# Gate's output row built through DRAM instead of on TensorE, later products with B, and two more tiles turned by VectorE and DMA

## The chip, the cores and the metric

The kernel runs on one core of a Trainium2 chip. The metric is the device time of one execution in microseconds (us). Five engines work beside each other, each through its own queue in order: TensorE (PE; its weight loads are listed as PEld), VectorE (DVE), ScalarE (ACT), GpSimd (POOL) and SyncE (SP), which here only issues DMAs. SBUF is the on-chip memory with 128 partitions; PSUM holds what TensorE accumulates.

## The reference

One layer of a hybrid trunk. 256 context tokens and 256 latent tokens are normalized, modulated and projected; one part of the projection feeds a bidirectional state-space scan (SSD), another a spatial-gating MLP. Both results go through one output projection, are normalized again, scaled by `g_post` and by the modulation's `gate`, and added to the input. Cut to what matters here:

```python
shift, scale, gate = split(silu(c) @ w_ada + b_ada, 3)
xbc = silu(dwconv(z[..., :4096]))          # x: 2048, B: 1024, C: 1024
xh, Bm, Cm = xbc as 32 heads x 64, 8 groups x 128, 8 groups x 128
# per group g and direction, chunks of 128 tokens
states = einsum('bckgn,bckgr,bckgrp->bcgrpn', Bc, decay_to_end, xdt)
CB     = einsum('bcqgn,bckgn->bcgqk', Cc, Bc)
y_diag = einsum('bcgqk,bcgrqk,bckgrp->bcqgrp', CB, Lmat, xdt)
y_off  = einsum('bcqgn,bcgrpn,bcqgr->bcqgrp', Cc, h_starts, exp(acs))
...
out = rmsnorm(mix_out(...), g_post)
x = x + gate[:, None] * out
```

## The kernel before

All products that need float32 accuracy are made of three matmuls: each weight is split into a rounded part (`hi`, by ACT, L87 and L543) and the rest (`lo`, by DVE, L88 and L549), and so is the activation (`hhi`, `hlo`).

**Stages.** First the modulation and the first seven tiles of the projection, while the normalized input is being made (to about 120 us in the profile). Then the loop over `REST`: 25 further tiles of 128 channels of x, B and C. Then 16 blocks of the projection for the latent tokens only (v, u, the two gates; L1219 to L1221, tile `pa`), then the output projection (`pm`, `pq`) and a tail.

**The 32 tiles.** Group g of the scan uses tiles 4g and 4g+1 (x), 4g+2 (B) and 4g+3 (C, latent tokens alone, so 256 columns where the others have 512). Tiles 0 to 3, 12, 13 and 15 are computed in the first stage and wait in PSUM or in `zq`. For the others PE fills one of two PSUM banks of `acp` (tile `psx`): 48 matmuls, 3 for each of 16 k. When a tile is complete, `conv_tile` reads the bank: ACT makes the first tap (L608), DVE the other four (L624, eight instructions for x and B, four for C), ACT the SiLU (L627). With two banks, a tile cannot start before DVE's last tap on the tile two before it. The names `xbc9`, `psx10` and so on carry the tile's number.

**Turning a tile.** x, B and the scan's result y have to be turned from channel-major to token-major. `by_pe` decides how. Either PE transposes four blocks of 128 by 128 into PSUM and ACT copies them (`ptx`, `ptb`, `pty`); or `turn` lets DVE transpose blocks of 32 by 32 (L739) and writes the result to DRAM (`Dx`, `Db`, `Dy`), and `turned` reads it back in four DMAs (`xk`, `bk`, `yz`, L747), all from SP's queue. Before, group 0 and, in group 7, everything but its first x tile go by PE.

**A group's tail.** `plan_tile` for a C tile plans the rest of the group: products of C with B (`pcb`) and states (`psc`, `psl`: B with the weighted x, `xw` and `xl`, from POOL) at +6, masks on DVE (`cbb`, `cbf`), start states (`hs`: ACT, then POOL, then DVE, L891), `M` and `E` per chunk (POOL, DVE), the product of C with the states (`pso`) at +12, `yo` (DVE), POOL's additions to y (L935), the diagonal product (`psy`) at +16, its turning (`yc`, `Dy`, `yz`) and the last addition. The next group's exponents (`E<-R`, L828) follow at +17; when they are read, `row_load` fetches the next `R`, a broadcast of 1 MB from `acs` in DRAM, from POOL's queue.

**What sets the order.** In the loops the order on PE, DVE, ACT and POOL is the program's own: `later(dt, fn)` puts a step into a list with a due time, and `pump(dt)` moves a clock on and issues what is due. A 512-column tile moves the clock by 10.4 units, eight times 1.3, each time after six matmuls; a 256-column tile by 5.2. `late` puts a group's tail off: 11 units where B is turned by DMA (14 for group 3). SP's queue and everything from the second latent block on are ordered by the framework's scheduler.

**Gate.** `gate_tile` (DVE) makes the 16 columns of gate, 128 values each. `gate_bcast` turns them into a row on all 128 partitions, `G`: it loads `g_post` as a broadcast, transposes gate on PE (`psgt`, L1095), splits it into two parts and spreads it in four matmuls (`pg`, L1105) with DVE's diagonal `gd` before and a product with `G` behind each. `G` is used at the very end (`o_gate`).

Of the kernel before, what the change touches and what calls it, by code (L numbers as in the profile page):

```python
# [20 lines left out]
NGRP = 8

FIRST = (0, 1, 2, 3, 12, 13, 15)
REST = tuple(i for i in range(32) if i not in FIRST)
NST = len(FIRST)
WST = 64 + NST * P

# [20 lines left out]
def tile_hybrid_ssd_mlp(  # L48
# [7 lines left out]
    pcols: bass.AP,  # L56
    dtp: bass.AP,
    dskip: bass.AP,
    gpost: bass.AP,
    gv: bass.AP,  # L60
    wst: bass.AP,
    wxbc: bass.AP,
# [5 lines left out]
    nc = tc.nc  # L68
# [5 lines left out]
    cpool = ctx.enter_context(mkpool(name="cpool", bufs=1))  # L74
# [21 lines left out]
    y = ypool.tile([P, 4, 2, 512], F32, tag="big16", name="y")  # L96
# [32 lines left out]
    bab = stp.tile([P, KT, 2], F32, name="bab")  # L129
    nc.vector.tensor_scalar(bab[:, :, 0], pc[:, C_BADA + 16 : C_BADA + 32], 1.0, None, op0=ALU.add)  # L130
    nc.vector.tensor_copy(bab[:, :, 1], pc[:, C_BADA : C_BADA + 16])
    gate = cpool.tile([P, 48], F32, name="gate")
    nc.gpsimd.memset(gate, 0.0)
    cpool.tile([P, 64], F32, name="cpad")

# [22 lines left out]
    zq = (yseg(2), yseg(3), yseg(7)[:, 0:256])  # L158
# [13 lines left out]
    def spt(shape, name):  # L172
        return sps.tile(shape, F32, tag="s", name=name)
# [10 lines left out]
    cb, cbj = (yseg(2), yseg(3)), yseg(0)  # L184
# [151 lines left out]
    for k in range(KT):  # L336
# [7 lines left out]
        g = k % 4  # L344
        nc.tensor.matmul(pss[32 * g : 32 * g + 32, :], lhsT=ones[:, 0:32], rhs=sq, start=k < 4, stop=k >= KT - 4)
        if g == 3:
# [7 lines left out]
                     start=True, stop=True)  # L354
# [161 lines left out]
    drp = ctx.enter_context(mkpool(name="drp", bufs=1, space=bass.MemoryType.DRAM))  # L516
# [204 lines left out]
    def row_load(g):  # L721
        if g >= NGRP:
            return
        R = cv1.tile([P, 4, 2, 2, P], F32, tag="R", name=f"R{g}")
        nc.gpsimd.dma_start(R.rearrange("p h d c q -> p (h d c q)"),
                            acs[4 * g : 4 * g + 4, :].rearrange("h x -> (h x)").unsqueeze(0).partition_broadcast(P))
        rows_[g] = R
# [5 lines left out]
        return ap.rearrange("p (h q) -> p h q", h=4)  # L733

    def by_pe(g, what):
        return g == 0 or g == NGRP - 1 and what != "x0"

    def turn(T, src, nm):
        nc.vector.transpose(T.rearrange("p (b g c) -> p g b c", b=4, g=4), src.rearrange("p (g b c) -> p g b c", g=4, b=4))  # L739
# [84 lines left out]
    def ssd_min(g, c):  # L824
        R = rows_[g]
        if c == 0:
            gs_.setdefault(g, {})["E"] = cv1.tile([P, 2, 4, P], F32, tag="E", name=f"E{g}")
        nc.vector.tensor_tensor(gs_[g]["E"][:, c], R[:, :, 0, c, :], R[:, :, 1, c, :], op=ALU.min)  # L828
        if c == 1:
            row_load(g + 1)  # L830

    def ssd_e(g):
        E = gs_[g]["E"]
# [140 lines left out]
    LAND = 4.5  # L974

    def plan_tile(i, src, d0=0.0, ds=5.2, tx=7.0, tw=1.5, late=0.0, td=0.0):

        g, r = divmod(i, 4)
        conv_tile(i, src, d0, ds)
        lx, lb, ly = (0.7 if by_pe(g, w) else LAND for w in (f"x{r}", "b", "y"))  # L980
        if lx == LAND:
            tw = max(tw, 2 * LAND + 3)
        if lb == LAND:
            late = max(late, 14.0 if i == 15 else 11.0)
        if r < 2:
# [33 lines left out]
    plan_tile(3, psx[3], 29, ds=5, late=2)  # L1019
    plan_d(17, 0, 1.3)  # L1020
    plan_e(22.5, 0)
    plan_tile(12, zq[0], 70, ds=7, tx=9)
    plan_tile(13, zq[1], 80, ds=7, tx=12.5)
    for n, i in enumerate(REST):
        lat = ORDER[i] >= 24
        ps = acp.tile([P, 256 if lat else 512], F32, tag="acc", name=f"psx{i}")
        for hf in range(2):
            whi, wlo = half(2 * n + hf)
            for kk in range(8):
                k = 8 * hf + kk  # L1030
                w = slice(kk * P, (kk + 1) * P)
                mm3(ps, whi[:, w], wlo[:, w], k, k == 0, k == KT - 1, lat)
                if kk % 2:
                    pump(0.65 if lat else 1.3)
        if i < 8:
            plan_tile(i, ps, ds=7, tx=11.5 if i == 4 else 9, tw=12, late=10)
        else:
            plan_tile(i, ps, td=1.3 if i < 12 else 0)
        if i == 14:
            plan_tile(15, zq[2], 8, late=10)  # L1040

# [33 lines left out]
    def gate_bcast():  # L1075
        gs.close()
        gp = ctx.enter_context(mkpool(name="gp", bufs=1, side="right"))
        G = gp.tile([P, D], F32, name="G")
        L_["G"] = G
        nc.gpsimd.dma_start(G, gpost.partition_broadcast(P))  # L1080
        nc.vector.tensor_tensor(gate[:, 0:16], gate[:, 0:16], pc[:, C_BADA + 32 : C_BADA + 48], op=ALU.add)
        nc.vector.tensor_copy(gate[:, 32:48], gate[:, 0:16])


        gh = gp.tile([48, P], F32R, name="gh")
        gl = gp.tile([48, P], F32R, name="gl")
        g1 = gp.tile([48, P], F32R, name="g1")
        gd = gp.tile([48, 4, P], F32R, name="gd")
        gk = gp.tile([48, KT], F32, name="gk")
        nc.scalar.copy(g1, ones[0:48])  # L1090
        nc.vector.tensor_tensor(gk, ident[0:48, 0:16], ident[0:48, 32:48], op=ALU.add)

        def rows():
            ps = spt([48, P], "psgt")
            nc.tensor.matmul(ps, lhsT=gate, rhs=ident, start=True, stop=True)  # L1095
            nc.scalar.copy(gh, ps)
            nc.vector.tensor_tensor(gl, ps, gh.bitcast(F32), op=ALU.subtract)
            nc.vector.tensor_copy(gh[32:48], gl[32:48].bitcast(F32))

        def expand(j):  # L1100
            nc.vector.tensor_tensor(gd, bc(gh.bitcast(F32), 1, 4), bc(gk[:, 4 * j : 4 * j + 4], 2, P), op=ALU.mult)

        def spread(j):
            p = spt([P, 512], f"pg{j}")
            nc.tensor.matmul(p, lhsT=g1, rhs=gd, start=True, stop=True)  # L1105
            gb = G[:, j * 512 : (j + 1) * 512]
            nc.vector.tensor_tensor(gb, p, gb, op=ALU.mult)
            if j < 3:
                expand(j + 1)

        later(2, rows)
        later(4, lambda: expand(0))
        for j in range(4):
            later(7 + 3 * j, lambda j=j: spread(j))
# [131 lines left out]
    G, yah, yal = L_["G"], L_["yah"], L_["yal"]  # L1246
# [121 lines left out]
    man.close()  # L1368


_INS = ["xch", "xtok", "ccols", "crow", "wada", "pcols", "dtp", "dskip", "gpost", "gv", "wst", "wxbc", "wlat", "wsp", "wout"]
_OUTS = [((256, 2048), "float32")]


def _layout(i):
    import numpy as np

    i = {k: np.asarray(v) for k, v in i.items()}
# [3 lines left out]
    a = {}  # L1382
# [4 lines left out]
    wada = np.empty((48, P, D), w_ada.dtype)  # L1387
# [5 lines left out]
    for m in range(NSING, KT, 2):  # L1393
# [5 lines left out]
    cb = i["conv_b"][0].reshape(32, P)[order].T  # L1399
    a["pcols"] = np.concatenate(  # L1400
        [i["b_ada"][0].reshape(48, P).T, i["g_pre"][0].reshape(KT, P).T, i["g_ssd"][0].reshape(KT, P).T,
         i["g_mlp"][0].reshape(KT, P).T, i["b_s"][0].T, cw, cb], axis=1)
    a["dtp"] = np.stack([i["dt_bias"][0].reshape(64), i["a_log"][0].reshape(64)])
    a["dskip"] = i["d_skip"].reshape(1, 32)
    a["gpost"] = i["g_post"].reshape(1, D)
    a["gv"] = i["g_v"].reshape(1, D)
    a["crow"] = c.reshape(1, D)
    wk = w_in.reshape(KT, P, -1)
# [35 lines left out]
```

## Time and profile before

| | |
|---|---|
| median of 3 runs | 968.88 us (967.64 to 969.93) |
| the profiled execution | 968.23 us, of which the span of the trace is 966.5 us |
| granted TensorE clock | 0.999 |
| busy time of POOL, the least loaded engine | 192.5 us, 20% of the span |
| moved by DMA | 224.57 MB in 141490 packets, 110816 of them under 512 B |

A row of the trace reads: start in us, duration in us, engine, line of the kernel, operation, written tile `<-` read tiles, shape, number of instructions (x4), and in square brackets how long the engine was idle before it and what ended that. Matmuls overlap: a row's duration is longer than the distance to the next start, so what a matmul costs is read from starts.

### The profile page before, as it was taken

What the parts mean: (1) busy time and instruction counts of PE and PEld (TensorE: products, weight loads), DVE (VectorE), ACT (ScalarE), POOL (GpSimd) and SP (SyncE); (2) the same over time, 40 slices, a digit from 0 to 9 for tenths busy, and PEclk for the clock granted to TensorE, in tenths of its full rate; (3) what the DMA queues carried; (4) which work ended last, traced back from release to release, by engine and by line L of the source; (5) the groups of instructions that cost most, each with busy time, mean ns of one, the idle gap of its engine ahead of it and who ended that gap; (6) DMA issues with size and microseconds to landing.
All of it is one profiled execution on the core that took longest, in us unless ns stands there. A gap on an engine that the chain in (4) does not pass through costs nothing.

```text
span 966.5 us, 13778 instructions
## 1 busy us (share of the span) xinstructions
PE 954.9 (99%) x5142; PEld 771.1 (80%) x5142; DVE 686.7 (71%) x1116; ACT 482.2 (50%) x732; POOL 192.5 (20%) x290
## 2 busy tenths in 40 slices
PE   9999999999999999999999999999999999999997
PEld 4688888777787878787888888887888888888885
DVE  6888798879887877866667687767666665445636
ACT  4344458554555544455445333455566564346512
POOL 0000002532533414323000000043335440000000
PEclk9999999999999999999999999999999999999999
DMA  9999965566659767647877767785666666556722
GB/s 367 416 416 415 371 228 166 145 187 156 136 151 229 170 179 163 164 143 248 317 295 281 285 259 273 285 302 197 198 226 214 215 214 216 198 181 255 261 87 87
DMA packets 141490, 224.57 MB, mean 232 GB/s; under 512 B 110816, under 2 KB 111072, under 8 KB 118768
## 3 DMA queue, kind: packets, MB, share of 16 engines
q1 hardware_dynamic: 134640, 206.03, 63.2%
q0 software_dynamic: 6208, 16.85, 5.6%
q8 instruction: 40, 0.66, 0.3%
q10 hardware_dynamic: 576, 0.82, 0.2%
q14 instruction: 26, 0.21, 0.1%
HBM read 210.76 MB, written 8.72 MB: 227 GB/s over the span
## 4 chain that ended last, share of the span: by engine, by line
PE 83%; DVE 7%; DMA 5%; issue 1%; SPq 1%; POOL 1%; ACT 1%; DVEq 0%; POOLq 0%; ACTq 0%
PE pa L1219 12%; PE pa L1220 12%; PE pa L1221 12%; PE psx L141 7%; PE psx L142 6%; PE psx L143 6%; PE pm L1260 3%; PE pm L1261 3%; PE pm L1262 3%; DMA ada<-in_wada_dram 3%; DVE xbc L624 3%; PE pq L1262 2%; PE pq L1260 2%; PE pq L1261 2%; PE psada L254 2%
## 5 line engine op out<-in xcount | busy, mean ns | idle before, releaser
L88 DVE TENSOR_TENSOR lo_w<-w,hi_w 128x1024 fp32r<-128x1024 f32 x173 | 210.5, 1222 | 138.1 <-ACT hi_w L87 137.9
L87 ACT CAST hi_w<-w 128x1024 fp32r<-128x1024 f32 x173 | 181.9, 1053 | 211.1 <-PE pa L1221 139.3
L1219 PE MATMUL pa<-hi_w,hhi 128*128 128x512 f32 x512 | 201.1, 393 | 0.0
L1221 PE MATMUL pa<-hi_w,hlo 128*128 128x512 f32 x512 | 199.3, 389 | 0.0
L1220 PE MATMUL pa<-lo_w,hhi 128*128 128x512 f32 x512 | 199.3, 389 | 0.0
L141 PE MATMUL psx<-hhi,hi_w 128*128 128x512 f32 (+1 forms) x400 | 151.5, 379 | 0.2 <-DVE xbc L624 0.2
L143 PE MATMUL psx<-hhi,lo_w 128*128 128x512 f32 (+1 forms) x400 | 145.7, 364 | 0.0
L142 PE MATMUL psx<-hlo,hi_w 128*128 128x512 f32 (+1 forms) x400 | 145.6, 364 | 0.0
L1219 PEld LDWEIGHTS pa<-hi_w,hhi 128*128 128x128 f32 x512 | 96.1, 188 | 21.2 <-issue 1.6
L1221 PEld LDWEIGHTS pa<-hi_w,hlo 128*128 128x128 f32 x512 | 96.1, 188 | 20.3
L1220 PEld LDWEIGHTS pa<-lo_w,hhi 128*128 128x128 f32 x512 | 96.1, 188 | 19.5 <-issue 0.2
L624 DVE SCALAR_TENSOR_TENSOR xbc<-psx,pc,xbc 128x248 f32<-128x248 f32 (+1 forms) x204 | 83.5, 473 | 26.0 <-ACT xbc L608 25.2
L549 DVE TENSOR_TENSOR lo_w<-w,hi_w 128x1024 fp32r<-128x1024 f32 x61 | 76.8, 1265 | 19.7 <-ACT hi_w L543 19.6
L141 PEld LDWEIGHTS psx<-hhi,hi_w 128*128 128x128 f32 x400 | 75.5, 189 | 14.8 <-issue 3.5
L142 PEld LDWEIGHTS psx<-hlo,hi_w 128*128 128x128 f32 x400 | 75.5, 189 | 12.9 <-issue 1.7
L143 PEld LDWEIGHTS psx<-hhi,lo_w 128*128 128x128 f32 x400 | 75.5, 189 | 12.3
L543 ACT CAST hi_w<-w 128x1024 fp32r<-128x1024 f32 x61 | 63.5, 1044 | 29.5 <-PE psx L142 16.6
L1260 PE MATMUL pm<-hi_w,hhi 128*128 128x512 f32 x128 | 49.8, 389 | 0.0
L1261 PE MATMUL pm<-lo_w,hhi 128*128 128x512 f32 x128 | 49.8, 389 | 0.0
L1262 PE MATMUL pm<-hi_w,hlo 128*128 128x512 f32 x128 | 49.8, 389 | 0.0
L1124 POOL DMA_DIRECT2D y<-T x64 | 36.8, 583 | 47.8 <-ACT sq L1195 33.1
L1124 POOL DMA_DIRECT2D vt<-T x64 | 36.8, 584 | 47.3 <-ACT sq L1195 34.8
(277 smaller groups left out, 1424.1 us busy)
## 6 DMA issues: line engine op xcount, KB each, us to landing
w<-in_wlat_dram SPq DMA_DIRECT2D x64, 1024.0 KB, 4.9
w<-in_wout_dram SPq DMA_DIRECT2D x32, 1024.0 KB, 4.8
w<-in_wxbc_dram SPq DMA_DIRECT2D x25, 1024.0 KB, 6.0
ada<-in_wada_dram SPq DMA_DIRECT2D x24, 1024.0 KB, 13.9
gate<-in_wada_dram SPq DMA_DIRECT2D x16, 1024.0 KB, 5.0
ada<-in_wada_dram SPq DMA_DIRECT2D x16, 512.0 KB, 12.4
R<-acs POOLq DMA_DIRECT2D x8, 1024.0 KB, 7.1
wst<-in_wst_dram SPq DMA_DIRECT2D x15, 480.0 KB, 13.0
```

What stands on the lines that cost most here:

```text
L87: nc.scalar.copy(hi, raw)
L88: nc.vector.tensor_tensor(lo, raw, hi.bitcast(F32), op=ALU.subtract)
L141: nc.tensor.matmul(ps, lhsT=whi, rhs=hhi[k][:, s], start=start, stop=False)
L142: nc.tensor.matmul(ps, lhsT=whi, rhs=hlo[k][:, s], start=False, stop=False)
L143: nc.tensor.matmul(ps, lhsT=wlo, rhs=hhi[k][:, s], start=False, stop=stop)
L624: nc.vector.scalar_tensor_tensor(ao, zi, cw[:, k : k + 1], ao, op0=ALU.mult, op1=ALU.add)
L1219: nc.tensor.matmul(pa[tk], lhsT=hhi[k][:, t], rhs=whi[:, w], start=k == 0, stop=False)
L1220: nc.tensor.matmul(pa[tk], lhsT=hhi[k][:, t], rhs=wlo[:, w], start=False, stop=False)
L1221: nc.tensor.matmul(pa[tk], lhsT=hlo[k][:, t], rhs=whi[:, w], start=False, stop=k == KT - 1)
L1260: nc.tensor.matmul(p, lhsT=yh[:, t], rhs=whi[:, w], start=j == 0, stop=False)
L1261: nc.tensor.matmul(p, lhsT=yh[:, t], rhs=wlo[:, w], start=False, stop=False)
L1262: nc.tensor.matmul(p, lhsT=yl[:, t], rhs=whi[:, w], start=False, stop=hf == 0 and j == 15)
```

## The change

Seven edits:

- `gate_bcast` no longer uses PE. `g_post` comes in as 16 more columns of `pc` and is multiplied into gate's 16 columns; DVE transposes these in blocks of 32 (`gt`); four small DMAs write them as one row to DRAM (`grow`), and one DMA reads that row back as a broadcast into `G`. The four are issued by POOL's queue, ahead of the first `vt<-T` of the second gate's turning.
- `by_pe`: group 0's first x tile and group 7's B tile are now turned by DVE and DMA.
- `REST`: tile 30 (B of the last group) comes before tiles 28, 29 and 31; its turning is planned 13 units behind its end.
- `late` is 14 instead of 11 units (17 instead of 14 for group 3), except in the last group, where it stays 0.
- Tile 12's convolution (x of group 3, held since the first stage) is planned 7 units earlier.
- `row_load` of group 5's `R` is put off by 12 units.
- `gate` shrinks from 48 to 32 columns, `pc` grows from 304 to 320.

```diff
-REST = tuple(i for i in range(32) if i not in FIRST)
+REST = tuple(i for i in range(28) if i not in FIRST) + (30, 28, 29, 31)
...
-    gate = cpool.tile([P, 48], F32, name="gate")
+    gate = cpool.tile([P, 32], F32, name="gate")
...
     def by_pe(g, what):
-        return g == 0 or g == NGRP - 1 and what != "x0"
+        return what != "x0" if g == 0 else g == NGRP - 1 and what in ("x1", "y")
...
         if c == 1:
-            row_load(g + 1)
+            later(12 if g == 4 else 0, lambda: row_load(g + 1))
...
-        if lb == LAND:
-            late = max(late, 14.0 if i == 15 else 11.0)
+        if lb == LAND and g < NGRP - 1:
+            late = max(late, 17.0 if i == 15 else 14.0)
...
-    plan_tile(12, zq[0], 70, ds=7, tx=9)
+    plan_tile(12, zq[0], 63, ds=7, tx=9)
...
-            plan_tile(i, ps, td=1.3 if i < 12 else 0)
+            plan_tile(i, ps, td=1.3 if i < 12 else 0, tx=13.0 if i == 30 else 7.0)
...
-        nc.gpsimd.dma_start(G, gpost.partition_broadcast(P))
         nc.vector.tensor_tensor(gate[:, 0:16], gate[:, 0:16], pc[:, C_BADA + 32 : C_BADA + 48], op=ALU.add)
-        nc.vector.tensor_copy(gate[:, 32:48], gate[:, 0:16])
...
-            ps = spt([48, P], "psgt")
-            nc.tensor.matmul(ps, lhsT=gate, rhs=ident, start=True, stop=True)
...
-            p = spt([P, 512], f"pg{j}")
-            nc.tensor.matmul(p, lhsT=g1, rhs=gd, start=True, stop=True)
-            gb = G[:, j * 512 : (j + 1) * 512]
-            nc.vector.tensor_tensor(gb, p, gb, op=ALU.mult)
...
+        nc.vector.tensor_tensor(gate[:, 0:16], gate[:, 0:16], pc[:, C_GPOST : C_GPOST + 16], op=ALU.mult)
+        gt = gp.tile([P, 32], F32, name="gt")
+        nc.vector.transpose(gt, gate)
+        row = drp.tile([16, P], F32, name="grow")
+        for a in range(4):
+            nc.gpsimd.dma_start(row[:, 32 * a : 32 * a + 32], gt[32 * a : 32 * a + 16])
+        nc.gpsimd.dma_start(G, row.rearrange("j p -> (j p)").unsqueeze(0).partition_broadcast(P))
```

**VectorE at the end of tile 10.** The names carry group or tile: `xbc10` is tile 10's convolution, `tx21` the turning of group 2's second x tile, `M11`, `E1`, `yo10`, `yc1` belong to group 1's tail, `E2` to the next group, `lo_w16` to a weight. Before:

```order
L549 TENSOR_TENSOR lo_w15_2206<-w7_1866,hi_w15_2182 128x1024
L905 SCALAR_TENSOR_TENSOR M11_2208<-cbf1_2144,dtt_1459,M11_2208 128x128 x4
L907 TENSOR_TENSOR E1_2079<-M11_2208,E1_2079 128x512
L927 TENSOR_TENSOR yo10_2235<-pso10_2210,ed_1460 128x512
L927 TENSOR_TENSOR yo11_2241<-pso11_2211,ed_1460 128x512
L549 TENSOR_TENSOR lo_w16_2277<-w8_1975,hi_w16_2254 128x1024
L739 STREAM_TRANSPOSE tx21_2279<-xbc9_2180 128x4x4x32
L739 STREAM_TRANSPOSE yc1_2283<-psy1_2262 128x4x4x32
L828 TENSOR_TENSOR E2_2287<-R2_2090 128x512 x2
L624 SCALAR_TENSOR_TENSOR xbc10_2312<-psx10_2173,pc_87,xbc10_2312 128x4x62
```

Now, at the same place:

```order
L623 SCALAR_TENSOR_TENSOR xbc12_2248<-y_68,pc_87,xbc12_2248 128x255
L623 SCALAR_TENSOR_TENSOR xbc12_2248<-y_68,pc_87,xbc12_2248 128x4x62
L623 SCALAR_TENSOR_TENSOR xbc12_2248<-y_68,pc_87,xbc12_2248 128x254
L738 STREAM_TRANSPOSE tx21_2266<-xbc9_2165 128x4x4x32
L926 TENSOR_TENSOR yo10_2270<-pso10_2231,ed_1460 128x512
L926 TENSOR_TENSOR yo11_2276<-pso11_2232,ed_1460 128x512
L738 STREAM_TRANSPOSE yc1_2307<-psy1_2298 128x4x4x32
L827 TENSOR_TENSOR E2_2311<-R2_2092 128x512 x2
L623 SCALAR_TENSOR_TENSOR xbc10_2320<-psx10_2158,pc_87,xbc10_2320 128x4x62
```

Tile 12's eight taps, which stood behind those of tile 10, now stand ahead of `tx21`, the two `yo`, `yc1`, `E2` and tile 10's taps. Ahead of them, between tile 9's taps and tile 12's, stand `hs1`, both `M` and both `E` of group 1 and two `lo_w`, where before `hs1`, `M10` and `E1` came ahead of tile 9's taps.

**TensorE at the end of tile 10.** `psy1` is group 1's diagonal product, `psx10` and `psx11` are tiles 10 and 11, `hi_w13` a weight. Before:

```order
L141 MATMUL psx10_2173<-hhi9_125,hi_w13_2056 128x512
L142 MATMUL psx10_2173<-hlo9_141,hi_w13_2056 128x512
L143 MATMUL psx10_2173<-hhi9_125,lo_w13_2087 128x512
L947 MATMUL psy1_2262<-E1_2079,xk1_1718 64x128 x8
L141 MATMUL psx10_2173<-hhi10_126,hi_w13_2056 128x512
L142 MATMUL psx10_2173<-hlo10_142,hi_w13_2056 128x512
```

Now:

```order
L140 MATMUL psx10_2158<-hhi15_131,hi_w13_2058 128x512
L141 MATMUL psx10_2158<-hlo15_147,hi_w13_2058 128x512
L142 MATMUL psx10_2158<-hhi15_131,lo_w13_2089 128x512
L946 MATMUL psy1_2298<-E1_2081,xk1_1720 64x128 x8
L140 MATMUL psx11_2313<-hhi0_116,hi_w14_2122 128x256
L141 MATMUL psx11_2313<-hlo0_132,hi_w14_2122 128x256
```

`psy1` moves from the middle of tile 10 (18 matmuls before its end) to behind its last matmul. `pcb1`, `psc1` and `psl1` move in the same way by 12 matmuls, from inside tile 9 to its end, and `pso1` by 18 in tile 10. The tails of groups 4, 5 and 6 move alike, with tiles 22, 26 and 29 in the place of 10; those of groups 2 and 3 too, behind tiles with other neighbours.

**SyncE in the last group.** `Db7` and `bk7` are the write and the reads of the last group's B, `Dx70` and `xk7` those of its first x tile, `Dy6` and `yz6` those of group 6's y; `w27` is a weight of 1 MB. Before:

```order
L741 DMA Dx70_3955<-tx70_3953 128x16x32
L81 DMA w27_4065<-in_wlat_dram 128x2048
L747 DMA xk7_3952<-Dx70_3955 32x16x32 x4
L81 DMA w28_4173<-in_wlat_dram 128x2048
L741 DMA Dy6_4099<-yc6_4097 128x16x32
L747 DMA yz6_4191<-Dy6_4099 32x16x32 x4
```

Now:

```order
L80 DMA w28_4168<-in_wlat_dram 128x2048
L740 DMA Db7_4008<-tb7_4006 128x16x32
L746 DMA bk7_4005<-Db7_4008 32x16x32
L740 DMA Dx70_4068<-tx70_4066 128x16x32
L746 DMA bk7_4005<-Db7_4008 32x16x32 x3
L740 DMA Dy6_4113<-yc6_4111 128x16x32
L746 DMA xk7_4065<-Dx70_4068 32x16x32 x4
L746 DMA yz6_4224<-Dy6_4113 32x16x32 x4
```

The five DMAs of B are new here, and the reads of `xk7` now stand behind `Dy6`, which waits for DVE's `yc6`.

More of the change, by code (lines that the diff above doesn't have):

```diff
@@ L36 @@
 WSSD = (0, 1, 2, 3, 4, 12, 5, 6, 13, 7, 8, 14, 9, 10, 15, 11)
-C_BADA, C_GPRE, C_GSSD, C_GMLP, C_BS, C_CW, C_CB, NPC = 0, 48, 64, 80, 96, 112, 272, 304
+C_BADA, C_GPRE, C_GSSD, C_GMLP, C_BS, C_CW, C_CB, C_GPOST, NPC = 0, 48, 64, 80, 96, 112, 272, 304, 320
 def _tile_order():
@@ L58, in tile_hybrid_ssd_mlp @@
     dskip: bass.AP,
-    gpost: bass.AP,
     gv: bass.AP,
@@ L1079, in gate_bcast @@
         L_["G"] = G
-        nc.gpsimd.dma_start(G, gpost.partition_broadcast(P))
         nc.vector.tensor_tensor(gate[:, 0:16], gate[:, 0:16], pc[:, C_BADA + 32 : C_BADA + 48], op=ALU.add)
-        nc.vector.tensor_copy(gate[:, 32:48], gate[:, 0:16])
[L1085 to L1093, printed above, removed]
-            ps = spt([48, P], "psgt")
-            nc.tensor.matmul(ps, lhsT=gate, rhs=ident, start=True, stop=True)
[L1096 to L1103, printed above, removed]
-            p = spt([P, 512], f"pg{j}")
-            nc.tensor.matmul(p, lhsT=g1, rhs=gd, start=True, stop=True)
-            gb = G[:, j * 512 : (j + 1) * 512]
-            nc.vector.tensor_tensor(gb, p, gb, op=ALU.mult)
[L1108 to L1114, printed above, removed]
+        nc.vector.tensor_tensor(gate[:, 0:16], gate[:, 0:16], pc[:, C_GPOST : C_GPOST + 16], op=ALU.mult)
[5 more added lines that the diff above has]
+        nc.gpsimd.dma_start(G, row.rearrange("j p -> (j p)").unsqueeze(0).partition_broadcast(P))
     def lat_t(kind, j4):
@@ L1368, in tile_hybrid_ssd_mlp @@
     man.close()
-_INS = ["xch", "xtok", "ccols", "crow", "wada", "pcols", "dtp", "dskip", "gpost", "gv", "wst", "wxbc", "wlat", "wsp", "wout"]
+_INS = ["xch", "xtok", "ccols", "crow", "wada", "pcols", "dtp", "dskip", "gv", "wst", "wxbc", "wlat", "wsp", "wout"]
 _OUTS = [((256, 2048), "float32")]
@@ L1401, in _layout @@
         [i["b_ada"][0].reshape(48, P).T, i["g_pre"][0].reshape(KT, P).T, i["g_ssd"][0].reshape(KT, P).T,
-         i["g_mlp"][0].reshape(KT, P).T, i["b_s"][0].T, cw, cb], axis=1)
+         i["g_mlp"][0].reshape(KT, P).T, i["b_s"][0].T, cw, cb, i["g_post"].reshape(KT, P).T], axis=1)
     a["dtp"] = np.stack([i["dt_bias"][0].reshape(64), i["a_log"][0].reshape(64)])
     a["dskip"] = i["d_skip"].reshape(1, 32)
-    a["gpost"] = i["g_post"].reshape(1, D)
     a["gv"] = i["g_v"].reshape(1, D)
```

## The prediction

> **What bounds the kernel now.** I read the page's busy times and chain first, then TensorE's own waits, then the timeline where the change touches it.
>
> ```profile
> PE 954.9 (99%) x5142; PEld 771.1 (80%) x5142; DVE 686.7 (71%) x1116; ACT 482.2 (50%) x732; POOL 192.5 (20%) x290
> ...
> PE 83%; DVE 7%; DMA 5%; issue 1%; SPq 1%; POOL 1%; ACT 1%; DVEq 0%; POOLq 0%; ACTq 0%
> ```
>
> ```profile
> PE psc L869 <- DMA bk<-Db: 2.8, 2, 1.4
> ...
> PE psx L141 <- DVE xbc L624: 0.2, 1, 0.2
> ```
>
> TensorE is busy for 99% of the span and waits for others little; between the first stage and the tail only for two products with B (2.8) and once for a PSUM bank (0.2). So a matmul taken from its queue is worth its full place there, a shorter op elsewhere nothing, and the question is whether another engine's new lateness makes TensorE wait.
>
> **Matmuls removed.** In an undisturbed stretch a 512-column matmul starts 0.227 after the last (143.92 to 144.37 is two steps). Where something is inserted I take two starts with one neighbour between them, less two steps (0.45).
>
> ```profile
> 143.92 0.39 PE L141 MATMUL psx<-hhi,hi_w 128*128 128x512 f32 x1
> 144.37 0.39 PE L143 MATMUL psx<-hhi,lo_w 128*128 128x512 f32 x1
> 144.60 0.60 PE L761 MATMUL ptx<-ident,xbc 128*128 128x128 f32 x4
> 145.27 0.39 PE L142 MATMUL psx<-hlo,hi_w 128*128 128x512 f32 x1
> ...
> 420.66 0.40 PE L1221 MATMUL pa<-hi_w,hlo 128*128 128x512 f32 x1
> 421.57 0.39 PE L1220 MATMUL pa<-lo_w,hhi 128*128 128x512 f32 x1
> ...
> 656.54 0.39 PE L1221 MATMUL pa<-hi_w,hlo 128*128 128x512 f32 x1
> 657.55 0.39 PE L1220 MATMUL pa<-lo_w,hhi 128*128 128x512 f32 x1
> ...
> 662.56 0.39 PE L1221 MATMUL pa<-hi_w,hlo 128*128 128x512 f32 x1
> 663.65 0.40 PE L1220 MATMUL pa<-lo_w,hhi 128*128 128x512 f32 x1
> ...
> 674.04 0.39 PE L1221 MATMUL pa<-hi_w,hlo 128*128 128x512 f32 x1
> 675.13 0.40 PE L1220 MATMUL pa<-lo_w,hhi 128*128 128x512 f32 x1
> ```
>
> Group 0's x tile (144.37 to 145.27, 0.90): 0.45. The last group's B (0.91): 0.46. Gate's transposition (1.01): 0.56. The first and the last `pg` (1.09 each): 0.64, times four 2.55. Together **4.0** off TensorE's queue. [...] Here the four rows together last 0.60 and overlap their neighbours, so the starts decide.
>
> **The two waits for B.** Each is the whole time by which `bk` landed late, at most 1.4. The products move by 12 matmuls, 12 x 0.227 = 2.7, and the chain to `bk` isn't put off: in group 2 tile 12's taps now stand ahead of tile 10's, not between them and `tb2`; in group 4 the rows are these:
>
> ```profile
> 291.86 0.59 POOL L725 DMA_DIRECT2D R<-acs  x1 [2.09 <-DVE E L828]
> 292.90 6.00 SPq L747 DMA_DIRECT2D bk<-Db  x4
> ```
>
> POOL's 1 MB broadcast was issued just ahead of the four reads, which took 6.00 to issue; it now comes 12 units later, behind them. `Dy3` now stands before `bk4` in SP's queue, but it needs about 18 from the start of group 3's tail, and `psc4` comes 33 after it, so 15 are left for a landing. Both waits go: **-2.8** (0 if the round trip grows by 1.3 or more).
>
> **What is late next.** `hs`, `M`, `E` and `yo` of six groups move to later places on DVE. Two things of TensorE depend on that: `pso`, and the tile after a 256-column tile, which needs the bank of the tile before that.
>
> ```profile
> 193.75 0.60 PE L852 MATMUL pcb<-xbc,xbc 128*128 128x128 f32 x4
> 196.58 0.58 PE L141 MATMUL psx<-hhi,hi_w 128*128 128x512 f32 x1
> 202.22 1.88 PE L921 MATMUL pso<-hs,xbc 128*128 128x512 f32 x4
> 203.54 0.79 PE L141 MATMUL psx<-hhi,hi_w 128*128 128x512 f32 x1
> ...
> 322.98 0.28 PE L141 MATMUL psx<-hhi,hi_w 128*128 128x256 f32 x1
> 328.73 0.40 PE L141 MATMUL psx<-hhi,hi_w 128*128 128x512 f32 x1
> ...
> 406.37 0.39 PE L143 MATMUL psx<-hhi,lo_w 128*128 128x512 f32 x1
> 407.71 0.50 PE L141 MATMUL psx<-hhi,hi_w 128*128 128x512 f32 x1
> ```
>
> ```profile
> 156.42 1.28 DVE L828 TENSOR_TENSOR E<-R 128x512 f32<-128x512 f32 x2
> ...
> 216.19 3.19 DVE L624 SCALAR_TENSOR_TENSOR xbc<-psx,pc,xbc 128x248 f32<-128x248 f32 x8 [3.13 <-ACT xbc L608]
> 219.53 0.47 PE L141 MATMUL psx<-hhi,hi_w 128*128 128x512 f32 x1 [0.22 <-DVE xbc L624]
> ...
> 304.74 0.39 DVE L860 TENSOR_TENSOR cbb<-pcb,tri_ge 128x256 f32<-128x256 f32 x1
> ...
> 307.30 1.00 DVE L891 TENSOR_TENSOR hs<-psl,hs 128x256 f32<-128x256 f32 x2 [0.51 <-POOL hs L885]
> ...
> 316.12 1.28 DVE L927 TENSOR_TENSOR yo<-pso,ed 128x512 f32<-128x512 f32 x2
> ...
> 319.86 1.83 DVE L828 TENSOR_TENSOR E<-R 128x512 f32<-128x512 f32 x2
> 320.07 1.07 POOL L935 TENSOR_TENSOR y<-y,yo 128x256 f32<-128x256 f32 x1
> ...
> 348.44 0.42 DVE L860 TENSOR_TENSOR cbb<-pcb,tri_ge 128x256 f32<-128x256 f32 x1 [0.46 <-PE pcb L852]
> ...
> 407.83 0.72 DVE L739 STREAM_TRANSPOSE yc<-psy 128x512 f32<-128x512 f32 x1 [0.18 <-PE psy L947]
> ```
>
> In the new order the tail starts at a tile's end; call that 0. The products take 2.83 (193.75 to 196.58), `pso` 1.32, 48 matmuls 10.9: tile 10 (or 22, 26, 29) ends at 15.0. `psy` adds 1.11 (1.34 between the starts less a step), the 256-column tile 5.75, so the next tile could start at 15.0 + 6.86. On DVE `yc` can start 1.23 after the tile's end (406.37 + 0.23 to 407.83) and hands on about 0.6 later; two `E<-R` take 1.28, the taps 3.19, and TensorE starts 0.15 after them (219.38 to 219.53): 6.45. The margin is **0.4**, provided that DVE is through `yo` by 16.2. From `cbb` to the end of `yo` the old order takes 12.66 (304.74 to 317.40) with the same pieces; the new one has one `lo_w` (1.1) and one `tx` (0.65) more ahead of `yc`, and `cbb` starts about 0.6 in: 15.1. So at tiles 22, 26 and 29 DVE waits for `psy`, and only POOL's additions, which run beside `E<-R`, eat the margin: with one of them beside it, it took 1.83 instead of 1.28. I take 0.2 at each of the three, **+0.6** (0 to 1.5).
>
> At tile 10 the eight taps of tile 12 (3.19) come ahead of `yc` too: 18.2, which is 2.0 late, less the margin 1.6, with a slow `E<-R` 1.9. In place of today's 0.2: **+1.7** (1.0 to 3.0).
>
> `pso` needs `hs`, which now has the taps and a `lo_w` ahead of it: 0.6 + 3.56 (304.74 to 308.30) + 3.1 + 1.1 = 8.4, while `pso` comes at 2.83 + 30 x 0.227 = 9.6. The margin is 1.2: nothing.
>
> **The other pieces.** Group 0's x tile costs DVE a transposition of 0.7 and gives ACT a copy back; DVE waited 2.9 soon behind that place, and SP had nothing to do between 144.8 and 155.4. The reads need two trips of some 4:
>
> ```profile
> Dx<-tx SPq DMA_DIRECT2D x13, 256.0 KB, 3.6
> xk<-Dx SPq DMA_DIRECT2D x52, 64.0 KB, 4.0
> ...
> 410.51 2.33 POOL L786 TENSOR_TENSOR xw<-xk,ed 128x256 f32<-128x256 f32 x4 [0.43 <-ACT xk L767]
> ```
>
> From 148.2 that lands near 156; POOL asks for it at 159.4. Nothing (if late: up to 1). In the last group it is now the x tile turned by TensorE that comes last: its transposes 12 matmuls into the first latent block, ACT's copy 1.2 after them, POOL's 2.33, and `psc` 18 matmuls and the products with C behind: about 1 to spare, and `xk7`, read behind `Dy6`, about 2. I take +0 (0 to 1). Gate's DMAs put the 16 issues of `vt<-T` off by some 3 to 5, for products tens of us away; DVE loses `gd` and the products with `G` (eight pieces of 0.7), where it has slack. Nothing.
>
> **Sum.** -4.0 - 2.8 + 1.7 + 0.6 = -4.5, on the profiled execution's 968.23 (the span's 966.5 and 1.7 around it): 963.7. That execution lies 0.65 under the median, so for the median 968.88 - 4.5 = **964.4**.
>
> **Rivals.**
> - *DVE keeps up everywhere.* Tile 10's wait stays at what it is and the three margins hold: -6.8, 962.1. For it: DVE was idle for 3.1 ahead of the taps at 216.19, because ACT held them up, and ACT's new order puts tile 10's first tap ahead of the exponents. Against: the 3.19 of tile 12 come into a stretch that is full.
> - *The waits for B stay.* The round trip moves with SP's queue, which waits for DVE: 964.4 + 2.8 = 967.2. Against: the broadcast is out of the way.
> - *DVE some 2 late at all four places*, because its taps share time with POOL: three places more at 1.4 to 2 each, about 968.5. The worst row says that it can be:
>
> ```profile
> 220.44 6.08 DVE L624 SCALAR_TENSOR_TENSOR xbc<-y,pc,xbc 128x248 f32<-128x248 f32 x8
> ```
>
>  Eight taps took 6.08 with POOL's `xw` and `xl` beside them, not 3.19. [...]
> - *Slower: `hs` too late in all six groups.* POOL's `M` and `hs` now run beside the taps that stand ahead of DVE's `hs`. It decides from about 2.4 of lateness: at 3.2, `pso` waits 2.0 in six groups, 12, and the four tile starts about 1 each: -6.8 + 12 + 4, about 978. Against: a margin of 1.2, and POOL's pieces there are short.
>
> **Chances.** The forecast 0.55 (963 to 966), the first rival 0.17, the second 0.08, the third 0.13, the last 0.07. The range 961.2 to 967.6 holds the first three and part of the third rival. About 0.2% (1.9) is what a measurement of this kernel can tell from no change: faster, under 966.9, is the forecast, the first rival and half a tenth of the next two, 0.77; same 0.13; slower 0.10.
>
> **What would show it.** `psgt`, `pg` and eight transposes gone from TensorE's rows; no wait of `psc` for `bk` in its list; one wait of `psx` for `xbc` near 220 of 1.5 to 2, and perhaps short ones near 328, 372 and 417. Wrong would be waits of `pso` for `hs`, or of `psc` for `xw` or `bk`, of more than 1.

## The result and the profile after

The changed kernel takes **961.91 us** (median of 6 runs, 961.66 to 962.48) where the kernel before takes 968.40 (6 runs, 967.56 to 969.93, the three that the forecast started from among them): a ratio of 0.9933, 95% interval 0.992 to 0.9946, or 5 to 8 us less. The forecast was 964.4, most likely 963 to 966, with 961.2 to 967.6 as its outer range. The profiled execution took 962.39, 5.84 less than that of before.

The page of the changed kernel, engines and chain:

```profile
PE 950.8 (99%) x5128; PEld 769.6 (80%) x5128; DVE 675.0 (70%) x1108; ACT 481.8 (50%) x728; POOL 192.1 (20%) x294
...
PE 93%; DVE 3%; DMA 2%; issue 1%; POOL 1%; ACT 0%; SPq 0%; POOLq 0%; ACTq 0%
```

TensorE's busy share is the same 99%; its chain share rose from 83% to 93%, since fewer detours over DVE and DMA end last. Its waits between 150 and 460 us are two, the first grown from 0.2, the second new:

```profile
PE psx L140 <- DVE xbc L623: 1.0, 1, 1.0
PE psc L868 <- POOL xw L785: 0.5, 1, 0.5
```

The waits for `bk` are gone; a wait for `xw` is there that the prediction had put at nothing, and the one at the start of tile 14 is 1.0, not 1.9. Where the 5.84 came from is read best by following one row through both traces. First the kernel before:

```profile
133.35 0.62 PE L705 MATMUL psa<-tri_le,y 128*32 128x128 f32 x4
...
155.95 0.60 PE L761 MATMUL ptx<-ident,xbc 128*128 128x128 f32 x4
...
523.09 1.95 PE L1169 MATMUL psg<-vt,gw 128*128 128x128 f32 x16
...
783.72 0.39 PE L1260 MATMUL pm<-hi_w,hhi 128*128 128x512 f32 x1
```

and the same four in the changed kernel:

```profile
133.39 0.62 PE L704 MATMUL psa<-tri_le,y 128*32 128x128 f32 x4
...
155.52 0.60 PE L760 MATMUL ptx<-ident,xbc 128*128 128x128 f32 x4
...
520.52 1.95 PE L1141 MATMUL psg<-vt,gw 128*128 128x128 f32 x16
...
777.95 0.39 PE L1232 MATMUL pm<-hi_w,hhi 128*128 128x512 f32 x1
```

The lead is -0.04 ahead of group 0's x tile, 0.43 behind it, 2.57 when the scan is over, 5.77 when gate is. So group 0's x tile gave 0.47, the scan of all groups 2.14, and gate 3.20. The 2.14 is itself a sum, which the waits resolve. The cost of one wait for `bk`, in the kernel before (from the products with C to the next tile matmul, group 2 and group 4):

```profile
238.69 0.60 PE L852 MATMUL pcb<-xbc,xbc 128*128 128x128 f32 x4
240.72 1.96 PE L869 MATMUL psc<-xw,bk 128*128 128x512 f32 x4 [1.42 <-DMA bk<-Db]
...
243.19 0.58 PE L141 MATMUL psx<-hhi,hi_w 128*128 128x512 f32 x1
...
301.70 0.60 PE L852 MATMUL pcb<-xbc,xbc 128*128 128x128 f32 x4
303.66 1.95 PE L869 MATMUL psc<-xw,bk 128*128 128x512 f32 x4 [1.35 <-DMA bk<-Db]
...
306.13 0.58 PE L141 MATMUL psx<-hhi,hi_w 128*128 128x512 f32 x1
```

In the changed kernel, group 2:

```profile
241.76 0.60 PE L851 MATMUL pcb<-xbc,xbc 128*128 128x128 f32 x4
...
244.60 0.58 PE L140 MATMUL psx<-hhi,hi_w 128*128 128x512 f32 x1
```

4.50 and 4.43 became 2.84. A wait of 1.42 cost 1.66, one of 1.35 cost 1.59: some 0.25 more than the idle time that the list of waits shows. Together 3.25, and B of the last group 0.46 (the run with it undone, below); against that stand 0.9 at tile 14 and 0.8 at the wait for `xw`, 0.54 and 0.27 around it. 0.47 + 0.46 + 3.20 + 3.25 - 0.9 - 0.8 is 5.7 of the 5.84. Tile 30's new place among the tiles was kept in every kernel that has the last group's edits, so it has no price of its own here.

### The profile page after: what moved, and what is told of

The parts are those of the page before. It is cut to its first block, busy times and chain, and to the rows that moved or that the text cites. A ratio compares the mean times of both kernels' runs of the same rounds, so it can differ in the third digit from the quotient of the medians.

```text
span 960.6 us, 13754 instructions
## 1 busy us (share of the span) xinstructions
PE 950.8 (99%) x5128; PEld 769.6 (80%) x5128; DVE 675.0 (70%) x1108; ACT 481.8 (50%) x728; POOL 192.1 (20%) x294
## 4 chain that ended last, share of the span: by engine, by line
PE 93%; DVE 3%; DMA 2%; issue 1%; POOL 1%; ACT 0%; SPq 0%; POOLq 0%; ACTq 0%
PE pa L1192 12%; PE pa L1191 12%; PE pa L1193 12%; PE psx L140 9%; PE psx L142 9%; PE psx L141 9%; PE pm L1232 3%; PE pm L1233 3%; PE pm L1234 3%; PE pq L1234 2%; PE pq L1232 2%; PE pq L1233 2%; PE psada L253 2%; DMA ada<-in_wada_dram 1%; PE pso L920 1%; PE psc L868 1%
## 5 line engine op out<-in xcount | busy, mean ns | idle before, releaser
L1071 DVE SCALAR_TENSOR_TENSOR junk<-gate,cb 128x2048 bf16<-128x2048 f32 x16 | 36.6, 2291 | 18.4 <-DMA gate<-in_wada_dram 18.4
```

## The experiments

Each kernel is timed beside the kernel before, whose runs had medians of 968.5 to 968.6 there.

**Gate alone.** The kernel before with the new `gate_bcast` (all of the diff's lines on gate and `pc`) and nothing else.

> The kernel before with gate's row over DRAM alone; everything else as before. Theory (each matmul taken from TensorE's queue is worth its place, nothing else moves): from the two traces the starts behind gate's products come 3.20 us earlier (2.57 to 5.77), so the time falls by 3.2, to some 965.3, and both waits of psc for bk stay (2.8). Rival 1 (part of the 5.8 that the profiled executions differ by is something else, such as the smaller gate tile or POOL's queue): the fall is under 2.6 or over 3.8. Rival 2 (the DMAs of the row delay vt<-T): a wait of psg or pa appears and the fall is under 2.5.

Measured: 965.70 (964.91 to 968.54), ratio 0.9966, 0.9955 to 0.9977. In its trace `psg` and `pm` of the rows above start at

```profile
523.72 1.95 PE L1141 MATMUL psg<-vt,gw 128*128 128x128 f32 x16
...
781.15 0.39 PE L1232 MATMUL pm<-hi_w,hhi 128*128 128x512 f32 x1
```

257.43 apart, where it was 260.63: 3.20 as expected; the medians give 2.9. The waits for `bk` stayed, at 1.79 and 1.98 in this execution, so they are not constant.

**The later tails alone.** The kernel before with

```diff
-            late = max(late, 14.0 if i == 15 else 11.0)
+            late = max(late, 17.0 if i == 15 else 14.0)
```

> The kernel before with the tails of groups 1 to 6 put off alone (14 and 17 for 11 and 14); tile 12 stays planned at 70 and the row of group 5 is not delayed. Theory A (putting the products off by 12 matmuls, 2.7, is enough for waits of 1.42 and 1.35): no psc waits for bk; each wait costs its length and some 0.25 in which TensorE gets back into step, so 3.2 less, and tile 14 waits no more than before (0.2): 965.2 or so. Rival B (the tail's pieces on DVE hold up the chain to bk as well, so it moves along with the products): one or both waits stay, and the time is 966.5 to 968.5. Rival C (the next tile waits for its bank behind the later yc): new waits of psx for xbc of 0.5 or more, 966 to 968.

Measured: 964.75 (964.55 to 965.64), ratio 0.9951, 0.9935 to 0.9968. TensorE waits neither for `bk` nor, at tile 14, for its bank. The time is theory A's, and this one line is worth 3.9 by the medians. But the products are not all that moved: VectorE also turns B sooner, in group 2 at 227.04 where the kernel before has 230.62. In group 4 the rows are, before and here:

```profile
289.08 0.70 DVE L739 STREAM_TRANSPOSE tb<-xbc 128x512 f32<-128x512 f32 x1
...
283.75 0.70 DVE L739 STREAM_TRANSPOSE tb<-xbc 128x512 f32<-128x512 f32 x1
```

By its issue and its time to landing, the last read of group 2's `bk` lands at 237.65 and not at 240.59, that of group 4's at 296.12 and not at 303.53 (some 2 of these 7.4 because TensorE is that far ahead by then). In group 2 VectorE no longer stands idle for 3.13 ahead of tile 10's taps, and tile 12's taps take 3.22 and not 6.08; in group 4 `yo` and an addition now stand behind the turning and not ahead of it.

**The later row of group 5 alone.** The kernel before with

```diff
-            row_load(g + 1)
+            later(12 if g == 4 else 0, lambda: row_load(g + 1))
```

> The kernel before with the broadcast of group 5's row put off by 12 units alone. Theory A (the 1 MB broadcast ahead of the four reads of group 4 is what made them take 6.00 to issue and land late): the wait of group 4's psc for bk goes, that of group 2 stays at 1.4; 1.6 less, some 966.8. Rival B (the reads are slow whatever POOL broadcasts, by weights in the same queues): the wait stays at 1 or more, and the time is that of the kernel before.

Measured: 968.93 (968.30 to 970.96), ratio 0.9999, 0.9989 to 1.0009. Theory A fell, and the time is rival B's. Its timeline around the four reads, the broadcast and the products:

```profile
293.06 2.40 SPq L747 DMA_DIRECT2D bk<-Db  x4
294.63 0.59 POOL L725 DMA_DIRECT2D R<-acs  x1
...
303.19 1.96 PE L869 MATMUL psc<-xw,bk 128*128 128x512 f32 x4 [0.98 <-DMA bk<-Db]
```

and the view of tile `bk` there, for the time from a read's issue to its landing:

```profile
DMA to landing us min/median/max: 5.7/6.9/8.9
```

The reads are issued in 2.40 now and not in 6.00, as the prediction wanted it, the last at 295.0 and not at 298.3, but the broadcast comes 1.6 behind their start, and they take up to 8.9 to land, where the last of before takes 5.2. The products start 0.47 sooner (303.19 for 303.66), and the wait is still 0.98. Where all four are issued ahead of the broadcast they land sooner: in the changed kernel they start at 288.47, the broadcast at 296.19, and they take 2.2 to 5.1. How much of the rest is due to a weight of 1 MB, which SyncE issues just ahead of the reads in both kernels (291.20 and 291.35), was not tried.

**The earlier tails back.** The changed kernel with 11 and 14 again, tile 12 and the row as changed.

> The changed kernel with the tails of groups 1 to 6 back at 11 and 14; tile 12 stays at 63 and group 5's row delayed. Theory A (in the changed kernel bk's reads in group 2 are issued from 232.19 on, not 234.46, because tile 12's taps stand earlier, and those of group 4 from 288.47 on, not 292.90; either alone is more than the waits of 1.42 and 1.35): the waits for bk stay away without the later tails, and tile 14's wait falls from 1.04 to under 0.3, since DVE gets through its tail sooner: 961 or less. Rival B (the later tails are what took the waits away): both waits come back, 2.8 and some 0.5 beside them, less the 0.8 of tile 14: 964.5.

Measured: 969.07 (967.94 to 970.59), ratio 1.0002, 0.9992 to 1.0011. Both theories fell in the time: there is no wait for `bk`, but the whole gain of the change was gone, with gate and two tiles still off TensorE. The timeline, ACT and DVE at tile 10's first tap, and TensorE at tile 14's start:

```profile
215.35 1.25 DVE L827 TENSOR_TENSOR E<-R 128x512 f32<-128x512 f32 x2
...
217.97 1.06 ACT L833 ACTIVATE E<-E 128x1024 f32<-128x1024 f32 x1
...
218.94 0.76 ACT L607 ACTIVATE xbc<-psx,pc 128x512 f32<-128x512 f32 x1
...
219.73 3.19 DVE L623 SCALAR_TENSOR_TENSOR xbc<-psx,pc,xbc 128x248 f32<-128x248 f32 x8 [3.13 <-ACT xbc L607]
...
223.07 0.77 PE L140 MATMUL psx<-hhi,hi_w 128*128 128x512 f32 x1 [3.80 <-DVE xbc L623]
...
223.64 0.63 PE L141 MATMUL psx<-hlo,hi_w 128*128 128x512 f32 x1
...
224.07 0.63 PE L142 MATMUL psx<-hhi,lo_w 128*128 128x512 f32 x1
```

With the early tails ACT's queue has tile 10's first tap behind the exponents, which wait for DVE's `E<-R`, and DVE then stands idle for 3.13. The kernel before has the same order on ACT and the same 3.13; but its `E<-R` starts at 211.22, since tile 12's taps stand behind it, and here at 215.35. So the wait there is 0.2 and here 3.80. In place of the changed kernel's 1.04, and with the slower matmuls behind it (last section), it makes 4.3 of the 6.3 by which the profiled execution, 968.70, is longer than the changed kernel's; the rest was not followed up. That no wait for `bk` is left says little, because TensorE comes 3.5 and 2.2 later to the two `psc` than in the kernel before. So tile 12 at 63 is only bearable with the later tails, which put the first tap ahead of the exponents (211.94 on ACT in the changed kernel).

**Tile 12 back at 70** in the changed kernel.

```diff
-    plan_tile(12, zq[0], 63, ds=7, tx=9)
+    plan_tile(12, zq[0], 70, ds=7, tx=9)
```

> The changed kernel with tile 12 planned at 70 again, and nothing else undone. Theory A (tile 12's eight taps, which stand on VectorE ahead of the copy of psy and of tile 10's taps, are all of the 1.04 that tile 14 waits; the later tails alone keep bk in time): no wait of psx for xbc; the 256-column tile and the wait behind it take 5.85 as in the run with the later tails alone, not 7.05: 1.2 less than the changed kernel's 961.9, so 960.7. Rival B (the earlier place was needed, since tile 12's taps now stand ahead of the transposition that bk of group 2 comes from): a wait of psc for bk of 0.5 to 1.4 in group 2, 961.5 to 962.4. Rival C (the wait is of the later tail itself): psx still waits 0.8 or more, 961.9.

Measured: 961.62 (961.01 to 961.81), ratio 0.9926, 0.9909 to 0.9942. The 256-column tile ahead of tile 14 and the first matmul behind it start at

```profile
213.05 0.39 PE L140 MATMUL psx<-hhi,hi_w 128*128 128x256 f32 x1
...
218.90 0.40 PE L140 MATMUL psx<-hhi,hi_w 128*128 128x512 f32 x1
```

5.85 apart, and in the changed kernel's trace 7.05:

```profile
212.85 0.39 PE L140 MATMUL psx<-hhi,hi_w 128*128 128x256 f32 x1
...
219.90 0.47 PE L140 MATMUL psx<-hhi,hi_w 128*128 128x512 f32 x1 [1.04 <-DVE xbc L623]
```

No wait for `bk` came back. The cause is the one that theory A names; but the medians differ by 0.3 and not 1.2, and the ranges overlap. A part of the reason is in the next run, another at the end of this section.

**Group 5's row at its old place** in the changed kernel.

> The changed kernel with group 5's row broadcast at its old place, as soon as group 4's E is made. Theory A (the later tails alone take group 4's wait away; the delay of the row by itself had taken at most 0.4 of it): no wait of psc for bk, time 961.9 as the changed kernel. Rival B (the delay is needed as well): a wait of psc for bk in group 4 of 0.3 or more, and 962.4 to 963.5.

Measured: 961.86 (961.72 to 962.08), ratio 0.9930, 0.9915 to 0.9945. No wait for `bk`: the later row is not needed beside the later tails. The reads start at 287.94 there and the broadcast at 293.37, behind the last of them, because the later tails have already moved both. And tile 14, where the 256-column tile starts at 212.93:

```profile
219.34 0.47 PE L140 MATMUL psx<-hhi,hi_w 128*128 128x512 f32 x1 [0.40 <-DVE xbc L623]
```

The wait is 0.40 here, and 0.39 to 0.40 in the three other runs that keep tile 12 at 63 and the later tails. The 1.04 is that of one execution, in which DVE began group 1's tail 1.3 behind the products (`cbb` at 197.38, products at 196.05) and not 0.6. By its usual size tile 12 costs 6.41 - 5.85 = 0.56, not 1.2.

**The last group's B by TensorE again**, in the changed kernel.

```diff
-        return what != "x0" if g == 0 else g == NGRP - 1 and what in ("x1", "y")
+        return what != "x0" if g == 0 else g == NGRP - 1 and what in ("x1", "b", "y")
```

> The changed kernel with the last group's B turned by TensorE again (four transposes back), still first of its tiles. Theory A (what stands behind the transposes moves along with them, the last x tile and the POOL products made of it too, so that the wait of psc for xw of 0.54 stays): 0.48 more than the changed kernel, as group 0's x tile measured, 962.4. Rival B (POOL's products come at their own pace, so the wait shrinks by what the transposes take): the wait falls to 0.1 and the time stays at 961.9; then the gain of the last group's B was given back at once to the wait for xw.

Measured: 962.16 (962.02 to 962.41), ratio 0.9933, 0.9918 to 0.9948. The wait for `xw` stays (0.53). Against the run just above, `psg` moved from 519.99 to 520.76; 0.31 of that stood there already before the last group, so 0.46 is the tile's. Theory A holds: what stands behind shifts along, and the removal keeps its worth.

**Group 0's x tile by TensorE again**, in the changed kernel.

> The changed kernel with group 0's first x tile turned by TensorE again. Theory A (four transposes and the stop around them are worth 0.48 on TensorE's queue, and nothing behind them waits): 0.5 more than the changed kernel's 961.9, 962.4, with the start of tile 4 0.45 to 0.5 later than in the changed kernel's trace. Rival B (the transposition on VectorE and its trip over DRAM cost something as well, in the full stretch before 160): under 0.2 more, 961.9 to 962.1.

Measured: 962.85 (962.30 to 963.27), ratio 0.9932, 0.9917 to 0.9948. In the trace the second x tile's transposes start at 156.10 with `psa` at 133.48, so 0.49 later than in the changed kernel. By the trace theory A holds; the median is 0.9 longer, in runs that lie 1 apart, and what makes up the other 0.4 is open.

**Both new waits taken away**: tile 12 at 70, and the last group's tail later,

```diff
         if lb == LAND and g < NGRP - 1:
             late = max(late, 17.0 if i == 15 else 14.0)
+        if i == 31:
+            late = 1.2
```

> The changed kernel with both of its new waits taken away: tile 12 planned at 70 again, and the tail of the last group put off by 1.2 units (six matmuls, 1.36, for a wait of 0.54). Theory A (the two waits are independent, 1.2 and 0.8 with the time TensorE takes to be back in step): 2.0 less than the changed kernel's 961.9, 959.9, and no wait of TensorE over 0.2 between the first stage and the tail. Rival B (one of them comes back elsewhere: bk of group 2, or what hangs on the later last tail): 960.7 to 961.9.

Measured: 961.75 (960.39 to 963.33), ratio 0.9929, 0.9914 to 0.9944. Both waits are gone from the trace, and the profiled execution, 960.39, is 2.0 under the changed kernel's, as expected; but the median misses the expected 959.9, and two of the four are at 962.73 and 963.33. Two more runs were to tell why, the last tail alone (tile 12 at 63):

> The changed kernel with the tail of the last group put off by 1.2 units alone; tile 12 stays at 63. Theory A (POOL's four xw are through 1.1 before the products then come): no wait of psc for xw, 0.8 less than the changed kernel, 961.1, with runs as close together as the changed kernel's (961.66 to 962.48). Rival B (the later last tail makes something behind it late in some executions, and that is why the kernel with both edits ran between 960.39 and 963.33): runs 2 or more apart here too.

Measured: 961.27 (960.90 to 961.92), ratio 0.9917, 0.9901 to 0.9932. And both edits once more:

> The kernel with both edits (tile 12 at 70, the last group's tail 1.2 later) once more, in more rounds. Theory A (its two long runs of four were disturbed by something outside the kernel): a median of 960 to 960.8 and all runs within 1. Rival B (one of its waits is there in some executions and not in others): runs between 960.3 and 963.4 again, a median near 961.5, and the profiled execution, if it is one of the long ones, shows a wait of TensorE of 1 or more between 200 and 450.

Measured: 961.25 (960.55 to 961.44), ratio 0.9917, 0.9901 to 0.9932. All runs are within 1, but the median is over the 960 to 960.8 of theory A. The nine executions with both edits have a median of 961.25. So the last tail is worth 0.6 or so, tile 12 perhaps 0.3; the intervals don't set either apart from the changed kernel. A part of what takes back the rest is in the trace of the run with the last tail alone, in the projection for the latent tokens, 130 us behind the edit:

```profile
555.58 2.29 DVE L1073 SCALAR_TENSOR_TENSOR junk<-gate,cb 128x2048 bf16<-128x2048 f32 x1 [3.33 <-DMA gate<-in_wada_dram]
...
559.07 0.50 PE L1194 MATMUL pa<-lo_w,hhi 128*128 128x512 f32 x1 [0.35 <-DVE lo_w L87]
```

TensorE waits there for a weight's `lo` part, which VectorE makes behind a product that had waited for a DMA, and loses 0.65 of its lead on the changed kernel at this place by the starts. With tile 12 alone at 70 the same place takes 0.35, so that of the usual 0.56 some 0.2 is left, near the 0.3 of the medians. In the profiled executions with both edits, the two fastest of their kernels, that product starts 1.1 or more sooner and nothing is lost. Whether this is what lengthens the other executions, which have no trace, is not shown.

## Why the prediction was right, and where it was off

| term | forecast | measured | from |
|---|---|---|---|
| gate's matmuls | -3.11 | -3.20 | two traces, gate alone |
| two tiles turned elsewhere | -0.91 | -0.93 | the traces; each undone |
| two waits for `bk` | -2.8 | -3.25 | starts in the two traces |
| tile 14 | +1.7 | +0.9 in the profiled execution, +0.3 in four others | starts |
| tiles 24, 30, block 0 | +0.6 | 0 | no wait there |
| wait for `xw` | 0 (0 to 1) | +0.8 | trace, last tail later |
| sum | -4.5 | -5.7, and -6.3 with tile 14 at its usual size | the profiled executions differ by 5.84, the medians by 6.49 |

**The matmuls** were right to 0.1: starts of the neighbours, not durations, give what an inserted group costs. The eight transposes are worth 0.93 by the traces (0.47 and 0.46), where a row of four lasts 0.60.

**The waits for `bk`** went, and the later tails alone take both away. The prediction gave two reasons. The first, products 12 matmuls (2.7) later while "the chain to `bk` isn't put off", is half of it: the same edit brings B sooner, its last read landing 2.9 and 7.4 earlier. Either is more than the waits of 1.42 and 1.35, they come by one line, and no run separates them. The second reason, "it now comes 12 units later, behind them", is a step that failed: the row's delay by itself shortens the reads' issue (2.40 for 6.00), leaves 0.98 of the wait and gains nothing in time (ratio 0.9999), and undone in the changed kernel it costs nothing. The size was low too: each wait takes TensorE 0.25 beside the idle time shown, and the waits differ between the traces that have them (1.35 to 1.98 without the row's delay). The runs of the changed kernel also lie closer together, 0.8 where those of before lie 2.4 apart; that this is due to these waits is not shown.

**Tile 14** is the term that was mis-sized most. The mechanism was right: the chain that ended last in the changed kernel runs through tile 12's eight taps, `yo`, `E<-R` and tile 10's taps, and with tile 12 back the wait is gone.

```profile
208.99 3.14 DVE xbc L623 x8
212.74 1.17 DVE yo L926 x2
214.54 2.11 DVE E L827 x2
216.65 2.43 DVE xbc L623 x7
```

Two steps of the sum failed, one on each engine. The first is DVE's 15.1 to the end of `yo`, 18.2 with tile 12's taps. In the run with the later tails alone, where the products start at 196.52, it is 14.1:

```profile
209.35 1.25 DVE L927 TENSOR_TENSOR yo<-pso,ed 128x512 f32<-128x512 f32 x2
```

The 12.66 of the old order were not "the same pieces": they held an addition of 0.71 (`y<-y,yz`) that group 1's tail doesn't have, and an `hs` of 1.00 that takes 0.75 here. So with tile 12 at 63 `yc` starts 17.15 behind the products in the four usual executions and 17.8 in the profiled one, which began late.

The second is "48 matmuls 10.9: tile 10 (or 22, 26, 29) ends at 15.0". It ended at 15.69 (196.05 to 211.51 and a step). The first matmul behind both inserted groups keeps the next one waiting longer than a step; in the changed kernel's timeline behind the products and behind `pso`:

```profile
198.89 0.58 PE L140 MATMUL psx<-hhi,hi_w 128*128 128x512 f32 x1
199.31 0.40 PE L141 MATMUL psx<-hlo,hi_w 128*128 128x512 f32 x1
...
207.20 0.79 PE L140 MATMUL psx<-hhi,hi_w 128*128 128x512 f32 x1
207.84 0.40 PE L141 MATMUL psx<-hlo,hi_w 128*128 128x512 f32 x1
```

0.42 and 0.64, not 0.227: 0.6 more room for DVE. The prediction quoted rows of 0.58 and 0.79 for just these matmuls, and reckoned them as 0.23 each. For the usual execution the terms then come out: 1.9 reckoned, less 1.05 for DVE, less 0.7 for tile 10 and 0.1 for the 256-column tile (5.85, not 5.75), and 0.5 more for the pieces behind `yc`, `E<-R` with its 2.19 above all: the measured 0.56.

**Tiles 24 and 30 and block 0** wait for nothing. Around tile 24:

```profile
317.32 3.05 POOL L934 TENSOR_TENSOR y<-y,yo 128x256 f32<-128x256 f32 x4 [4.31 <-DVE yo L926]
...
320.07 0.72 DVE L738 STREAM_TRANSPOSE yc<-psy 128x512 f32<-128x512 f32 x1 [2.23 <-PE psy L946]
320.71 1.25 DVE L827 TENSOR_TENSOR E<-R 128x512 f32<-128x512 f32 x2
321.88 3.19 DVE L623 SCALAR_TENSOR_TENSOR xbc<-psx,pc,xbc 128x248 f32<-128x248 f32 x8
...
325.81 0.40 PE L140 MATMUL psx<-hhi,hi_w 128*128 128x512 f32 x1
```

DVE waits for `psy` as said, but POOL's additions are over when `E<-R` starts: 1.25 for the two, not 1.83. The taps end at 325.07 and the tile starts at 325.81, a margin of 0.6 where 0.4 was said. At these three tiles the disturbance that was to eat it doesn't come; it does at tile 10, where DVE is late and `E<-R` took 2.19 beside POOL's additions.

**The wait for `xw`** was seen as "about 1 to spare", from a row in which POOL's four took 2.33. In the changed kernel they stand beside DVE's making of weight parts:

```profile
418.59 2.77 DVE L548 TENSOR_TENSOR lo_w<-w,hi_w 128x1024 fp32r<-128x1024 f32 x2
...
418.74 5.22 POOL L785 TENSOR_TENSOR xw<-xk,ed 128x256 f32<-128x256 f32 x4 [9.49 <-ACT xk L766]
...
424.01 1.12 PE L868 MATMUL psc<-xw,bk 128*128 128x512 f32 x2 [0.54 <-POOL xw L785]
```

The four took 5.22, 2.9 more than reckoned, and 1 to spare became a wait. It is only 0.54 because the first two of the four `psc` go ahead, at 422.45. The prediction told of longer ops beside each other on DVE's side (6.08 for 3.19) and left them out on POOL's.

The time lies 2.5 under the forecast, below its 963 to 966. Among the rivals, it is that of "DVE keeps up everywhere" (962.1), and by the medians nearly its terms: three margins held and tile 14 usually waits 0.4. But the agreement is partly chance, since the wait for `xw` and the low price of the waits for `bk` were in neither. "The waits for B stay" and `hs` too late for `pso` didn't come; no `pso` waited.

## What to carry to other kernels

Price a wait, and an inserted group of other products, by the distance between starts of the matmuls around it, not by the idle time or by the durations: here 0.25 more for a wait and 0.2 to 0.4 more behind each of two groups, and both decide margins of half a microsecond. When several edits aim at one wait, run each alone: here one number (11 to 14) took both waits away, the later row did nothing, and the earlier tile 12 cost 0.56. And when an op of GpSimd is moved beside VectorE's, take its duration from a row where VectorE works too: here 2.33 became 5.22.

## What had not been expected of the hardware

**The wait of 3.80 was followed by slow matmuls.** In the run with the earlier tails, it is followed by matmuls 0.43 apart and not 0.227 (223.64 to 224.07 above). In a stretch of that trace (length; busy time and instructions of PE, PEld, DVE, ACT, POOL; granted clock; DMA share; GB/s):

```profile
223.00:227.00 4.00, 3.93 (x11) 3.17 (x12) 3.93 (x6) 2.43 (x4) 2.67 (x4) 0.58 0.61 95
```

The granted clock is 1.00 in the 4 us that hold the wait, 0.58 in the 4 us behind it, and 1.00 again in the next 4. The first step behind it took 0.57, six more 0.42 to 0.43, the next 0.33: some 1.6 more than at 0.227 each. The clock of 0.58 says much the same, 0.42 of 4 us being 1.7, and the mean over the span is 0.997. Waits up to 1.98 show nothing of the kind: in the kernel before the clock is 1.00 in the 4 us behind the waits of 1.42 and 1.35, and in the run with gate alone, with 1.79 and 1.98, it is 0.999 over the span. How long a wait it takes, and whether the wait is the cause, is not shown by this one trace. By these runs the prediction's slower case, with waits of 2.0, would hardly have met it. The kernel before may meet it at times: of the 41 executions of it that were timed beside the experiments, the nine of 970 us and more show a granted clock of 0.996 to 0.998, the other 32 of 0.998 to 0.999, and 1.7 us lost, as there, lower the mean over the span by 0.002. None of the nine was traced, so which wait it would be is not shown.

**VectorE's and GpSimd's ops took longer beside each other**, both ways: `E<-R` 1.25 alone and 2.19 beside POOL's additions, which took 3.85 there and 3.05 apart; POOL's `xw` 2.33 in the kernel before, with VectorE idle, and 5.22 beside DVE's weight parts. The prediction's own row at 319.86 shows 0.55 more for `E<-R` beside an addition of 1.07.
